# A conformer block on one core: the first feed-forward's up projection by seven block products, and its modulation vectors loaded later

## Chip, cores and metric

One core of a Trainium2 chip runs the kernel in one launch. The metric is device microseconds; the time of a kernel is the median over its runs. Rows of the profile come from one further execution, whose own time is given beside its span.

## What is computed

One layer on x of 512 tokens by 1024 features, all in float32 accuracy:

```python
ada = silu(c) @ w_ada + b_ada                # 9 modulation vectors of 1024
(sh1, sc1, g1, sh2, sc2, g2, sh3, sc3, g3) = split(ada, 9)
h = rmsnorm(x, ffn1_norm) * (1 + sc1) + sh1
x = x + 0.5 * g1 * swiglu(h, ffn1_w_in, ffn1_w_out)      # swiglu: (silu(h @ wg) * (h @ wu)) @ w_out
h = rmsnorm(x, mix_norm) * (1 + sc2) + sh2
z = h @ w_in      # latents of an MLA attention | q, k, v of a chunked attention | two gates
x = x + g2 * ((sigmoid(gA) * (mla @ w_branch_a) + sigmoid(gB) * (chunk @ w_branch_b)) @ w_out)
h = rmsnorm(x, ffn2_norm) * (1 + sc3) + sh3
x = x + 0.5 * g3 * swiglu(h, ffn2_w_in, ffn2_w_out)
return rmsnorm(x, final_norm)
```

The feed-forward is 2816 wide, so each up projection has 22 blocks f of 128 gate and 128 up columns. Vectors are counted 0 to 8 in the order above: 0 and 1 serve the first feed-forward, 2 is its gate; 4 and 3 are the mixer's scale and shift, 5 its gate; 7, 6 and 8 belong to the second feed-forward.

## The kernel before

**Products.** Every operand of a matmul is split into a high part (a cast on ACT, `split`, L196) and a low part (a subtraction on DVE, L197; in the mixer often on POOL), and every product is three matmuls, hi·hi, lo·hi, hi·lo (`mm3`, L212 to L214). Weights come as loads of 128x1024 (512 KB) into `raw`, a ring of five buffers, issued on SP's queue in the program's order (L191); their parts stand in a ring `wh`, `wl`.

**Stages.** The program goes through: the start, where vectors 0 and 1, the norm and F0 = 3 up blocks are made (`first_units`, order of all engines written by hand); the other 19 up blocks of the first feed-forward; its down projection; the mixer's norm; the mixer (latents, two attentions of 8 heads each, gates, output); the norm; two plain and 20 fast up blocks of the second feed-forward; its down projection and the last norm. Behind the start TensorE's order is the order of the code; the order of the other engines comes from a scheduler that goes by priorities, and each engine takes its instructions strictly in that order.

**Up blocks.** In the first feed-forward (`ffn_up`) a block is two units of 8 steps x 3 matmuls of 512 columns, 48 matmuls; behind each block `swiglu` (L502, L503) makes the activation and splits it at once. In the second one 20 blocks go through `up_fast`: the block matrix product of 2x2 in seven products instead of eight, 7 x 4 x 3 = 84 matmuls of 256 columns. Later products are added to PSUM sums that an ACT copy has seeded. Its price per block stands on DVE and ACT: three sums of weights (L612, L613, L616), splits of the sums, four copies and two silu (L624 to L638), three combinations (L632, L634, L641). It needs sums of the tokens too (`mix_tokens`). A third of its loads uses two free buffers of the gate rows and one of `ada`. Its activations stay unsplit and are split by `act_parts` in the down stage.

**Modulation vectors.** A vector is eight loads of 512 KB from `w_ada`, each followed by one DVE instruction: `ada_dot` (L287, with a short read) for shift and scale, `ada_step` (L283, adds to `ada_acc`) for a gate; a gate ends with `ada_rows` (a split, four matmuls with `ones`, L310 and L311, two ACT copies, L312). Vectors 2, 4, 3, 7, 6, 5 are streamed through the first up stage, one or two steps for each of 38 units; vector 8 through the second down stage.

**The mixer.** `Fill` hands out pieces of projection matmuls between the steps of the attention heads (`Head`, L74 to L107: a score bank, DVE L81, ACT exponential L83, DVE L84 and L85, transposes, a split by ACT L96 and DVE L97, values).

Of the kernel before, what the change touches and what calls it, by code (L numbers as in the profile page):

```python
# [18 lines left out]
P = 128  # L19
# [22 lines left out]
EARLY_UP, FLUSH_UP = 3, (0, 2)  # L42
F2 = 2
FLUSH_LAT = {0: 2, 1: 1}
# [75 lines left out]
class Fill:  # L120
    def __init__(self, ahead):
        self.jobs, self.ready, self.run, self.ahead = [], [], None, ahead

# [8 lines left out]
    def __call__(self, n):  # L132
        while n > 0:
            if self.run is None:
                self.look(1)
                if not self.ready:
                    return
                run, units = self.ready.pop(0)
                self.run = run(units)
                self.look(self.ahead)  # L140
            try:
                next(self.run)
                n -= 1
            except StopIteration:
                self.run = None
# [5 lines left out]
class Block:  # L151
# [115 lines left out]
    def mix_tokens(self, j):  # L267
        nc = self.nc
        ha, hb = self.mixed[2 * j:2 * j + 2]
        if not j:  # L270
            self.sums = [[self.slot([P, KT // 2, S // 2], F32R, "sum_" + p) for p in "hl"] for _ in range(4)]
        a11, a12, a21, a22 = (h[:, ks] for h in (ha, hb) for ks in (slice(0, 4), slice(4, 8)))
        tt = nc.vector.tensor_tensor
# [4 lines left out]
        cs = slice(j * P, (j + 1) * P)  # L278
        for (h, l), part in zip(self.sums, (a22, a11, a21, a12)):
            self.split(part, h[:, :, cs], l[:, :, cs])  # L280

# [32 lines left out]
    def ada_gate(self, vec):
        io, nc = self.io, self.nc
        layer = vec // 3
        acc = self.main.tile([P, D], F32, tag="ada", name="ada_acc", bufs=1)
        nc.gpsimd.memset(acc, 0.0)
        nc.scalar.dma_start(acc[0:1], io["b_ada"][:, vec * D:(vec + 1) * D])
        for j in range(KT):  # L320
            self.ada_step(acc, j, self.raw(D, io["w_ada"][vec, j]))
            yield j == KT - 1
        self.gate[layer] = self.fix.tile([P, D], F32, tag="gate", name="gate_bc", bufs=2)
        self.ada_rows(acc, self.gate[layer])
        yield True
# [50 lines left out]
    def first_units(self):  # L376
# [121 lines left out]

    def swiglu(self, psg, psu):
        nc = self.nc  # L500
        sc = self.sc4((P, 2, S))
        nc.scalar.activation(sc[:, 0], psg, AF.Silu)  # L502
        nc.vector.tensor_tensor(sc[:, 1], sc[:, 0], psu, op=ALU.mult)  # L503
        act = self.slot([P, 2, S], F32R, "act")
        self.split(sc[:, 1], act[:, 0], act[:, 1])
        return act

    def ffn_up(self, w1, fs, side):
        jobs = [(f, gu) for f in fs for gu in range(2)]
        ps, units, acts = {}, {}, []  # L510

        def mms(job, ns):
            hi, lo = units[job]
            for k in range(KT):
                cs = slice(k * P, (k + 1) * P)
                self.mm3(ps[job][:, ns], (hi[:, cs], lo[:, cs]), (self.hH[:, k, ns], self.hL[:, k, ns]),
                         k == 0, k == KT - 1)

        for i, job in enumerate(jobs):
            f, gu = job  # L520
            units[job] = self.unit(D, w1[f, gu])
            ps[job] = self.bank("o" if f % 2 and gu else "mm")
            mms(job, slice(0, S))
            while len(acts) < len(fs) and (fs[len(acts)], 1) in ps:
                n = fs[len(acts)]
                acts.append(self.swiglu(ps[n, 0], ps[n, 1]))
            side(i)
        return acts

    def act_tile(self, f):  # L530
# [3 lines left out]

    def up_plain(self, w1, fs, early, flush):
        nc = self.nc
        jobs = [(f, gu) for f in fs for gu in range(2)]
# [10 lines left out]
        for i, job in enumerate(jobs):  # L548
# [3 lines left out]
            if i < early:  # L552
# [5 lines left out]
                for late in jobs[:early]:  # L558
                    mms(late, S // 2, S)
                self.mix_tokens(0)  # L560
            else:
                mms(job, 0, S)
                if i == early:
                    self.mix_tokens(1)
            while done < len(fs) and (fs[done], 1) in ps:
                n = fs[done]
                sc = self.sc4((P, S))
                nc.scalar.activation(sc, ps[n, 0], AF.Silu)
                nc.vector.tensor_tensor(self.act_tile(n), sc, ps[n, 1], op=ALU.mult)
                done += 1  # L570

    def up_fast(self, w1, fs):
        nc = self.nc
# [22 lines left out]
        def load(n, i, src):  # L596
            m = (2 * n + i) % 7
# [310 lines left out]
    def mix(self, after):  # L908
        nc = self.nc
        self.fill = Fill(2)  # L910
# [139 lines left out]
    def layer(self, banks):  # L1050
        nc, io = self.nc, self.io
        acts = [self.swiglu(banks[2 * i], banks[2 * i + 1]) for i in range(F0)]
        self.rope_angles()
        gen = self.vectors((2, 4, 3, 7, 6, 5))
        acts += self.ffn_up(io["w1a"], range(F0, NF), lambda i: self.advance(gen, 1 + i % 2))
        for _ in range(3):
            self.advance(gen, 99)

        parts = lambda u: [[acts[2 * u + j][:, i] for i in range(2)] for j in range(2)]
        self.down(parts, NF, io["w2a"], 0, 3, lambda t, xn: self.norm_token(t, 1, xn), LAG_DOWN)  # L1060
        self.mix(lambda t, xn: self.norm_token(t, 2, xn))
# [33 lines left out]
def pack(inputs):  # L1095
# [17 lines left out]
    for tag, n in (("a", "ffn1"), ("b", "ffn2")):  # L1113
        w1 = a[n + "_w_in"][0].reshape(KT, P, 2, NF, P)
        both = w1.transpose(3, 2, 1, 0, 4).reshape(NF, 2, P, D)
        if tag == "b":
            q = w1.reshape(2, 4, P, 2, NF, P).transpose(4, 0, 3, 2, 1, 5)
            fast = np.stack([np.stack([q[:, 0, 0], q[:, 1, 1]], 2), np.stack([q[:, 1, 0], q[:, 0, 1]], 2)], 1)
            both = np.concatenate([both[:F2], fast.reshape(NF, 2, P, D)[F2:]])
        out["w1" + tag] = c(both)  # L1120
# [46 lines left out]
```

## Time and profile before

| | us |
|---|---|
| median of 3 runs (1115.17 to 1118.07) | 1115.86 |
| the profiled execution | 1115.35 |
| its span | 1113.6 |
| TensorE busy | 1084.4 |
| DVE busy | 700.7 |
| ACT busy | 525.1 |
| POOL busy | 134.7 |

Times inside the span are us from its start. TensorE's granted clock is full in all 40 slices of the span. "Busy" of an engine is time with an instruction in work; a matmul of 512 columns starts every 0.233 us, though its row shows 0.39, since matmuls overlap.

### The profile page before, as it was taken

Reading aid. Unit: us, or ns where it says so; the run is one execution under the profiler, and the core shown is the slowest. Engines: PE = TensorE matmul, PEld = TensorE weight load, DVE = VectorE, ACT = ScalarE, POOL = GpSimd, SP = SyncE. Lnnn points to the kernel's source line nnn. Section 1 sums busy time; section 2 is a strip of 40 time slices with the busy share of each in tenths; the row PEclk is TensorE's granted clock in tenths of the full one; section 3 lists DMA queues with packets and bytes.
Section 4 is the critical chain, followed back from the end, with each engine's and each line's share of the span. In section 5 each row is a group of like instructions: output and inputs, shape, how many; then the busy total and the mean of one; then the engine's idle time right before and its main releaser. Section 6 shows DMA issues by size and latency. Waiting matters only on the chain.

```text
span 1113.6 us, 15325 instructions
## 1 busy us (share of the span) xinstructions
PE 1084.4 (97%) x5884; PEld 925.4 (83%) x5884; DVE 700.7 (63%) x1170; ACT 525.1 (47%) x963; POOL 134.7 (12%) x126
## 2 busy tenths in 40 slices
PE   4999999999999999999999999999999999999997
PEld 3788888888888898988888788888999999988885
DVE  5887565663232575766677832459888787785724
ACT  5533232223122486766656633337555555654512
POOL 1000000000000011333343445100000000000100
PEclk9999999999999999999999999999999999999999
DMA  9677666663333630112222233623333333374312
GB/s 361 230 256 248 212 219 214 199 214 117 95 95 94 204 113 21 57 58 67 76 92 80 67 114 94 207 97 116 113 114 97 100 108 114 115 248 131 95 57 76
DMA packets 42993, 149.85 MB, mean 135 GB/s; under 512 B 5156, under 2 KB 5156, under 8 KB 42919
## 3 DMA queue, kind: packets, MB, share of 16 engines
q1 hardware_dynamic: 38160, 136.20, 37.3%
q10 hardware_dynamic: 4758, 12.66, 3.2%
q8 instruction: 46, 0.75, 0.3%
q14 instruction: 29, 0.23, 0.1%
HBM read 142.55 MB, written 6.29 MB: 134 GB/s over the span
## 4 chain that ended last, share of the span: by engine, by line
PE 90%; DVE 4%; ACT 3%; DMA 1%; issue 1%; ACTq 0%; POOLq 0%
PE ps_mm L212 14%; PE ps_mm L213 14%; PE ps_mm L214 14%; PE ps_s L213 3%; PE ps_s L214 3%; PE ps_s L212 3%; PE ps_o L214 3%; PE ps_o L212 3%; PE ps_o L213 3%; PE ps_s L586 3%; PE ps_s L587 3%; PE ps_s L588 3%; PE ps_t L212 2%; PE ps_t L214 2%; PE ps_t L213 2%; PE ps_t L586 2%
## 5 line engine op out<-in xcount | busy, mean ns | idle before, releaser
L196 ACT CAST wh<-raw 128x1024 fp32r<-128x1024 f32 x154 | 161.7, 1051 | 255.7 <-PE ps_t L214 73.5
L197 DVE TENSOR_TENSOR wl<-raw,wh 128x1024 fp32r<-128x1024 f32 x122 | 149.3, 1225 | 125.4 <-ACT wh L196 124.9
L212 PE MATMUL ps_mm<-h_hi,wh 128*128 128x512 f32 (+1 forms) x464 | 180.5, 389 | 0.0
L214 PE MATMUL ps_mm<-h_hi,wl 128*128 128x512 f32 (+1 forms) x464 | 177.9, 384 | 2.0 <-DVE wl L197 2.0
L213 PE MATMUL ps_mm<-h_lo,wh 128*128 128x512 f32 (+1 forms) x464 | 177.8, 383 | 0.2 <-DVE h_lo L197 0.2
L214 PEld LDWEIGHTS ps_mm<-h_hi,wl 128*128 128x128 f32 x464 | 87.2, 188 | 21.1 <-DVE wl L197 2.2
L213 PEld LDWEIGHTS ps_mm<-h_lo,wh 128*128 128x128 f32 x464 | 87.4, 188 | 16.3 <-DVE h_lo L197 0.4
L212 PEld LDWEIGHTS ps_mm<-h_hi,wh 128*128 128x128 f32 x464 | 87.4, 188 | 16.0
L197 POOL TENSOR_TENSOR wl<-raw,wh 128x1024 fp32r<-128x1024 f32 x32 | 77.1, 2413 | 81.2 <-ACT wh L196 81.2
L287 DVE CUSTOM_DVE_ANT_0 raw<-raw,c_row,cols_sb 128x1024 f32<-128x1024 f32 x32 | 41.0, 1284 | 46.5 <-DMA raw<-w_ada 46.4
L219 POOL TENSOR_TENSOR rstd<-ss,neghalf 128x1 f32<-128x1 f32 x16 | 10.4, 648 | 408.1 <-DVE ss L229 398.4
L83 ACT ACTIVATE sc<-sc,stat 128x128 f32<-128x128 f32 (+1 forms) x64 | 35.9, 562 | 29.2 <-DVE stat L81 29.0
L586 PE MATMUL ps_t<-sum_h,wh 128*128 128x256 f32 x160 | 44.8, 280 | 0.0
L588 PE MATMUL ps_t<-sum_h,wl 128*128 128x256 f32 x160 | 44.7, 279 | 0.0
L587 PE MATMUL ps_t<-sum_l,wh 128*128 128x256 f32 x160 | 44.7, 279 | 0.0
L587 PE MATMUL ps_s<-sum_l,wh 128*128 128x256 f32 x160 | 44.7, 279 | 0.0
L588 PE MATMUL ps_s<-sum_h,wl 128*128 128x256 f32 x160 | 44.7, 279 | 0.0
L586 PE MATMUL ps_s<-sum_h,wh 128*128 128x256 f32 x160 | 44.7, 279 | 0.0
L97 DVE TENSOR_TENSOR pt<-ps_t,pt 128x512 fp32r<-128x512 f32 (+1 forms) x64 | 30.9, 488 | 16.5 <-ACT pt L96 15.6
L283 DVE SCALAR_TENSOR_TENSOR ada_acc<-raw,cact,ada_acc 128x1024 f32<-128x1024 f32 x24 | 30.8, 1283 | 16.6 <-DMA raw<-w_ada 16.6
L196 ACT CAST act<-sc 128x512 fp32r<-128x512 f32 x22 | 13.6, 622 | 57.3 <-DVE sc L503 57.3
L197 DVE TENSOR_TENSOR act_l<-act,act_h 128x1024 fp32r<-128x1024 f32 x22 | 27.9, 1273 | 17.0 <-PE ps_t L213 15.9
(404 smaller groups left out, 2884.0 us busy)
## 6 DMA issues: line engine op xcount, KB each, us to landing
raw<-w_ada SPq DMA_DIRECT2D x56, 512.0 KB, 4.3
raw<-w1a SPq DMA_DIRECT2D x38, 512.0 KB, 4.2
raw<-w1b SPq DMA_DIRECT2D x28, 512.0 KB, 3.5
raw<-w2a SPq DMA_DIRECT2D x22, 512.0 KB, 3.5
raw<-w2b SPq DMA_DIRECT2D x22, 512.0 KB, 3.5
w_first<-w_first SPq DMA_DIRECT2D x16, 512.0 KB, 9.3
raw<-w_gate SPq DMA_DIRECT2D x16, 512.0 KB, 3.6
raw_g<-w1b SPq DMA_DIRECT2D x11, 512.0 KB, 3.5
```

Source lines behind the costliest of these rows:

```text
L83: nc.scalar.activation(p, p, AF.Exp, scale=-1.0, bias=low, accum_out=tot)
L97: nc.vector.tensor_tensor(pl[:, :n], pt[:, :n], ph[:, :n].bitcast(F32), op=ALU.subtract)
L196: nc.scalar.copy(hi, src)
L197: (low_engine or nc.vector).tensor_tensor(lo, src, hi.bitcast(F32), op=ALU.subtract)
L212: mm(ps, lh, rh, start=start, stop=False)
L213: mm(ps, lh, rl, start=False, stop=False)
L214: mm(ps, ll, rh, start=False, stop=stop)
L283: self.nc.vector.scalar_tensor_tensor(acc, w, self.cact[:, j:j + 1], acc, op0=ALU.mult, op1=ALU.add)
L287: self.nc.vector.tensor_tensor_reduce(w, w, self.c_row, 1.0, self.cols[:, b:b + 1], ALU.mult, ALU.add, out)
L586: mm(ps, hi[:, cs], lh, start=start and k == 0, stop=False, skip_group_check=not start)
L587: mm(ps, hi[:, cs], ll, start=False, stop=False, skip_group_check=not start)
L588: mm(ps, lo[:, cs], lh, start=False, stop=k == 3, skip_group_check=not start)
```

## The change

Of the first feed-forward's 19 up blocks two stay plain and 17 go through `up_fast`; the plain ones now use `up_plain`, and `mix_all` makes the token sums from `h32`, the modulated tokens, which are kept in the buffer that held x. So x is loaded a second time (`x_again`, four loads on ACT's queue) before the down stage, and its activations are split in the down stage by `act_parts`. In this `up_fast` loads use the five `raw` buffers for four in five and `ada` for one in five. Vector 2 is accumulated in its gate row, with one step behind each fast block from the sixth on; vectors 4 and 3 move to the down stage, one step for each of its units; vectors 7, 6 and 5 move to the mixer, one step at the start of each of Fill's jobs. `ada_rows` takes its split buffers from `wh` and `wl`. For vector 2 the DMA of its bias (L338 of the changed kernel) is issued in the start.

```diff
-F2 = 2
+F1, F2 = 2, 2
+WEIGHTS_A = ("raw",) * 4 + ("ada",)
+WEIGHTS_B = ("raw",) * 4 + ("gate",) * 2 + ("ada",)
...
-    def __init__(self, ahead):
-        self.jobs, self.ready, self.run, self.ahead = [], [], None, ahead
+    def __init__(self, ahead, side):
+        self.jobs, self.ready, self.run, self.ahead, self.side = [], [], None, ahead, side
...
+                self.side()
...
+    def sum_tiles(self):
+        self.sums = [[self.slot([P, KT // 2, S // 2], F32R, "sum_" + p) for p in "hl"] for _ in range(4)]
+
+    def mix_all(self):
+        self.sum_tiles()
+        h = self.halves(self.h32)
+        parts = [h[:, ks, :, b] for b in range(2) for ks in (slice(0, 4), slice(4, 8))]
+        self.token_sums(*parts, [[z.rearrange("p k (a c) -> p k a c", a=2) for z in pair] for pair in self.sums])
...
+    def gate_row(self, name="gate_bc"):
+        return self.fix.tile([P, D], F32, tag="gate", name=name, bufs=2)
+
+    def ada_rows(self, acc):
+        nc = self.nc
+        hi, lo = (self.ring.tile([P, D], F32R, tag="w" + p, name="gate_" + p) for p in "hl")
...
-            nc.scalar.mul(out[:, cs], ps, 0.5)
+            nc.scalar.mul(acc[:, cs], ps, 0.5)
...
-        acc = self.main.tile([P, D], F32, tag="ada", name="ada_acc", bufs=1)
+        if layer not in self.gate:
+            self.gate[layer] = self.gate_row()
+        acc = self.gate[layer]
...
-        self.gate[layer] = self.fix.tile([P, D], F32, tag="gate", name="gate_bc", bufs=2)
-        self.ada_rows(acc, self.gate[layer])
+        self.ada_rows(acc)
...
-        self.c_row = self.fix.tile([P, D], F32, tag="gate", name="c_row", bufs=2)
+        self.gate[0] = self.gate_row()
+        self.c_row = self.gate_row("c_row")
...
-            h32 = self.sc4((P, S)) if k < KT - 1 else self.main.tile([P, S], F32, tag="ada", name="h32", bufs=1)
+            h32 = self.h32[:, k]
...
+        self.h32 = self.fix.tile([P, KT, S], F32, tag="x16", name="h32")
...
-    def up_fast(self, w1, fs):
+    def up_fast(self, w1, fs, homes, side=None):
...
-            if m < 4:
+            home = homes[(2 * n + i) % len(homes)]
+            if home == "raw":
                 return self.raw(D, src)
-            if m < 6:
-                tile_ = self.fix.tile([P, D], F32, tag="gate", name="raw_g", bufs=2)
-            else:
-                tile_ = self.main.tile([P, D], F32, tag="ada", name="raw_a", bufs=1)
+            tile_ = self.gate_row("raw_g") if home == "gate" else self.main.tile([P, D], F32, tag="ada", name="raw_a", bufs=1)
...
+            if side:
+                side(n)
...
+        gen = self.vectors((7, 6, 5))
+        self.fill = Fill(2, lambda: self.advance(gen, 1))
         merged = self.attention()
+        for _ in range(3):
+            self.advance(gen, 99)
         self.low_engine = nc.vector
         self.x = self.fix.tile([P, NT, D], F32, tag="x16", name="x_back")
...
-        acts = [self.swiglu(banks[2 * i], banks[2 * i + 1]) for i in range(F0)]
+        self.acts = []
+        for f in range(F0):
+            self.swiglu(f, banks[2 * f], banks[2 * f + 1])
         self.rope_angles()
-        gen = self.vectors((2, 4, 3, 7, 6, 5))
-        acts += self.ffn_up(io["w1a"], range(F0, NF), lambda i: self.advance(gen, 1 + i % 2))
-        for _ in range(3):
-            self.advance(gen, 99)
-
-        parts = lambda u: [[acts[2 * u + j][:, i] for i in range(2)] for j in range(2)]
-        self.down(parts, NF, io["w2a"], 0, 3, lambda t, xn: self.norm_token(t, 1, xn), LAG_DOWN)
+        self.up_plain(io["w1a"], range(F0, F0 + F1), {0: self.mix_all})
+        gen = self.vectors((2,))
+        self.up_fast(io["w1a"], range(F0 + F1, NF), WEIGHTS_A, lambda n: self.advance(gen, n > 4))
+        self.x = self.fix.tile([P, NT, D], F32, tag="x16", name="x_again")
+        for t in range(NT):
+            nc.scalar.dma_start(self.x[:, t], io["x"][t * P:(t + 1) * P])
+        late = self.vectors((4, 3))
+        self.down(self.act_parts, NF, io["w2a"], 0, 3, lambda t, xn: self.norm_token(t, 1, xn), LAG_DOWN,
+                  side=lambda hf, u: self.advance(late, 1))
...
-        self.up_fast(io["w1b"], range(F2, NF))
-        fin = self.fix.tile([P, D], F32, tag="gate", name="final_gain", bufs=2)
+        mixes = {EARLY_UP + j - 1: lambda j=j: self.mix_tokens(j) for j in range(2)}
+        self.up_plain(io["w1b"], range(F2), mixes, EARLY_UP, FLUSH_UP)
+        self.up_fast(io["w1b"], range(F2, NF), WEIGHTS_B)
+        fin = self.gate_row("final_gain")
         nc.scalar.dma_start(fin, io["final"].to_broadcast([P, D]))
```

The host packs w1a accordingly (blocks from the sixth on in the order that `up_fast` reads).

Three places show the order of engines. The first is VectorE in the first up stage. Before (one plain block, with steps of vector 7, `adac`):

```order
165 L503 TENSOR_TENSOR sc_1122<-sc_1122,ps_mm 128x512
166 L197 TENSOR_TENSOR wl<-raw,wh 128x1024
167 L197 TENSOR_TENSOR act<-sc_1122,act 128x512
168 L287 ISA raw,adac<-raw,c_row,cols_sb 128x1024
169 L287 ISA adac 128x1
170 L197 TENSOR_TENSOR wl<-raw,wh 128x1024
171 L287 ISA raw,adac<-raw,c_row,cols_sb 128x1024
172 L287 ISA adac 128x1
```

The changed kernel, one fast block with a step of vector 2 (L297, the former L283); L599, L600 and L603 are the sums of weights, L619, L621 and L628 the combinations:

```order
203 L619 TENSOR_TENSOR sc_1781<-ps_t,sc_1781 128x256
204 L200 TENSOR_TENSOR wl<-raw,wh 128x1024
205 L200 TENSOR_TENSOR wl<-w_sums,wh 128x1024
206 L621 TENSOR_TENSOR sc_1781<-ps_s,sc_1781 128x256
207 L200 TENSOR_TENSOR wl<-raw,wh 128x1024
208 L628 TENSOR_TENSOR act<-sc_1781,sc_1872 128x2x2x128
209 L297 SCALAR_TENSOR_TENSOR gate_bc<-raw,cact,gate_bc 128x1024
210 L200 TENSOR_TENSOR w_last<-w_sums,w_last 128x512 x2
211 L599 TENSOR_TENSOR w_sums<-raw,raw_a 128x1024
```

The step stands ahead of the low part `w_last` of the next block and of the sums of the block behind it.

The second place is ScalarE where the up stage ends. Before, behind the last silu of the up stage (L502) come the casts for the down stage, whose activation halves are split already:

```order
129 L196 CAST wh<-raw 128x1024
130 L312 ACTIVATE gate_bc<-ps_t 128x512 x2
131 L502 ACTIVATE sc_1975<-ps_mm 128x512
132 L196 CAST wh<-raw 128x1024
133 L196 CAST act<-sc_1975 128x512
134 L196 CAST wh<-raw 128x1024 x10
```

The changed kernel (`sc_2747` belongs to the last block; L624 and L625 are its two silu):

```order
222 L1053 DMA x_again<-x 128x1024 x2
223 L618 COPY ps_o<-ps_s 128x256
224 L624 ACTIVATE sc_2747<-ps_mm 128x256
225 L1053 DMA x_again<-x 128x1024
226 L625 ACTIVATE sc_2747<-ps_o 128x256
227 L199 CAST wh<-raw 128x1024 x3
228 L199 CAST act_h<-act 128x1024 x3
```

The first weight of the down stage is now cast behind the second silu, which reads the last product's PSUM.

The third place is VectorE in the mixer, at the end of a head of the first attention. Before:

```order
468 L81 ISA sc_3683,stat<-ps_s,masks 128x512
469 L81 ISA stat 128x1
470 L84 RECIPROCAL stat<-stat 128x1
471 L85 TENSOR_SCALAR sc_3683<-sc_3683,stat 128x512
472 L114 TENSOR_TENSOR o_3213<-ps_o,o_3213 64x512
473 L968 TENSOR_TENSOR kT<-ps_t,kT 64x512
474 L978 TENSOR_TENSOR qT<-ps_t,qT 96x512
```

The changed kernel at the end of such a head, where vector 7 is finished (its last step is L301, the former L287):

```order
561 L83 ISA sc_4609,stat<-ps_s,masks 128x512
562 L83 ISA stat 128x1
563 L301 ISA raw,adac<-raw,c_row,cols_sb 128x1024
564 L301 ISA adac 128x1
565 L86 RECIPROCAL stat<-stat 128x1
566 L313 SCALAR_TENSOR_TENSOR scale_83<-adac,cols_sb 128x8
567 L87 TENSOR_SCALAR sc_4609<-sc_4609,stat 128x512
568 L116 TENSOR_TENSOR o_4130<-ps_o,o_4130 64x512
569 L960 TENSOR_TENSOR kT<-ps_t,kT 64x512
570 L970 TENSOR_TENSOR qT<-ps_t,qT 96x512
```

The step moved into the place where VectorE waits for the exponential, ahead of the reciprocal.

## Rows read from the trace of the kernel before

**Rows 1.** The page's first part: busy us, share of the span, instructions.

```profile
PE 1084.4 (97%) x5884; PEld 925.4 (83%) x5884; DVE 700.7 (63%) x1170; ACT 525.1 (47%) x963; POOL 134.7 (12%) x126
```

**Rows 2.** Windows: stretch, length, busy us by engine, clock, DMA share, GB/s.

```profile
57.20:271.80 214.60, 214.60 (x921) 172.94 (x920) 135.35 (x184) 66.35 (x89) 0.95 (x1) 1.00 0.65 213
271.80:388.00 116.20, 116.20 (x499) 93.51 (x498) 40.71 (x50) 31.31 (x41) 0.55 (x1) 1.00 0.37 116
437.00:650.00 213.00, 209.52 (x1179) 178.57 (x1178) 150.26 (x391) 140.41 (x329) 78.08 (x69) 1.00 0.22 70
861.00:881.00 20.00, 20.00 (x171) 19.77 (x170) 16.11 (x21) 11.36 (x20) 0.00 (x0) 1.00 0.36 104
```

**Rows 3.** Timeline of PE in the first up stage: start, us, instruction.

```profile
57.18 0.39 PE L212 MATMUL ps_mm<-h_hi,wh 128*128 128x512 f32 x1
...
96.38 0.39 PE L310 MATMUL ps_t<-sc,ones 128*128 128x512 f32 x1
...
271.83 0.40 PE L212 MATMUL ps_s<-wh,act 128*128 128x512 f32 x1
```

**Rows 4.** Timeline of PE: first and last fast matmul, start of the second down stage.

```profile
781.23 0.28 PE L586 MATMUL ps_s<-h_hi,wh 128*128 128x256 f32 x1
...
980.44 0.28 PE L588 MATMUL ps_o<-h_hi,w_last 128*128 128x256 f32 x1
...
981.95 0.50 PE L213 MATMUL ps_s<-wl,act_h 128*128 128x512 f32 x1 [0.76 <-DVE wl L197]
```

**Rows 5.** Groups by form, whole span: busy us, mean ns | idle before.

```profile
L197 DVE TENSOR_TENSOR wl<-raw,wh 128x1024 fp32r<-128x1024 f32 x122 | 149.3, 1225 | 125.4 <-ACT wh L196 124.9
L287 DVE CUSTOM_DVE_ANT_0 raw<-raw,c_row,cols_sb 128x1024 f32<-128x1024 f32 x32 | 41.0, 1284 | 46.5 <-DMA raw<-w_ada 46.4
L283 DVE SCALAR_TENSOR_TENSOR ada_acc<-raw,cact,ada_acc 128x1024 f32<-128x1024 f32 x24 | 30.8, 1283 | 16.6 <-DMA raw<-w_ada 16.6
...
L196 ACT CAST wh<-raw 128x1024 fp32r<-128x1024 f32 x154 | 161.7, 1051 | 255.7 <-PE ps_t L214 73.5 <-issue 62.5 <-PE ps_o L214 53.6
L638 ACT ACTIVATE sc<-ps_o 128x256 f32<-128x256 f32 x20 | 7.7, 384 | 7.4 <-PE ps_o L588 7.3
```

**Rows 6.** Timeline of DVE in a fast block, with PE's at 872.

```profile
869.16 1.23 DVE L197 TENSOR_TENSOR wl<-w_sums,wh 128x1024 fp32r<-128x1024 f32 x1 [0.17 <-ACT wh L196]
...
872.34 0.28 PE L586 MATMUL ps_t<-sum_h,wh 128*128 128x256 f32 x1
```

**Rows 7.** Start: piece of the chain that ended last; ACT's queue at 55.

```profile
8.03 1.06 ACT c_row L450
...
54.97 0.49 ACTq L319 DMA_DIRECT2D ada_acc<-b_ada  x1
```

**Rows 8.** DMA issues: KB each, median us to landing.

```profile
raw<-w_ada SPq DMA_DIRECT2D x56, 512.0 KB, 4.3
```

**Rows 9.** Timelines of POOL, DVE and PE in the mixer, from 447 to 639.

```profile
447.45 1.87 DVE L85 TENSOR_SCALAR sc<-sc,stat 128x512 f32<-128x512 f32 x1
...
480.42 4.74 POOL L197 TENSOR_TENSOR wl<-raw,wh 128x1024 fp32r<-128x1024 f32 x2 [5.37 <-ACT wh L196]
...
483.06 2.31 DVE L85 TENSOR_SCALAR sc<-sc,stat 128x384 f32<-128x384 f32 x1
...
485.76 0.39 PE L107 MATMUL ps_o<-pt,vs 128*128 128x256 f32 x1 [1.48 <-DVE pt L97]
...
579.38 2.39 POOL L197 TENSOR_TENSOR wl<-raw,wh 128x1024 fp32r<-128x1024 f32 x1
...
579.65 2.67 DVE L197 TENSOR_TENSOR o_hl<-o,o_hl 128x512 fp32r<-128x512 f32 x1 [0.18 <-ACT o_hl L196]
...
608.45 0.69 DVE L197 TENSOR_TENSOR o_hl<-o,o_hl 128x512 fp32r<-128x512 f32 x1 [0.69 <-ACT o_hl L196]
...
638.19 1.33 DVE L85 TENSOR_SCALAR sc<-sc,stat 128x256 f32<-128x256 f32 x1
```

**Rows 10.** Waits, 437 to 650: total us, times, longest.

```profile
DVE stat L84 <- ACT sc L83: 17.5, 27, 1.4
```

More of the change, by code (lines that the diff above doesn't have):

```diff
@@ L267, in mix_tokens, with token_sums @@
     def mix_tokens(self, j):
-        nc = self.nc
         ha, hb = self.mixed[2 * j:2 * j + 2]
         if not j:
-            self.sums = [[self.slot([P, KT // 2, S // 2], F32R, "sum_" + p) for p in "hl"] for _ in range(4)]
+            self.sum_tiles()
         a11, a12, a21, a22 = (h[:, ks] for h in (ha, hb) for ks in (slice(0, 4), slice(4, 8)))
-        tt = nc.vector.tensor_tensor
+        cs = slice(j * P, (j + 1) * P)
+        self.token_sums(a11, a12, a21, a22, [[z[:, :, cs] for z in pair] for pair in self.sums])
+    def token_sums(self, a11, a12, a21, a22, out):
+        tt = self.nc.vector.tensor_tensor
         tt(a22, a21, a22, op=ALU.add)
@@ L277, in mix_tokens @@
         tt(a12, a12, a11, op=ALU.subtract)
-        cs = slice(j * P, (j + 1) * P)
-        for (h, l), part in zip(self.sums, (a22, a11, a21, a12)):
-            self.split(part, h[:, :, cs], l[:, :, cs])
+        for (hi, lo), part in zip(out, (a22, a11, a21, a12)):
+            self.split(part, hi, lo)
+    def sum_tiles(self):
+        self.sums = [[self.slot([P, KT // 2, S // 2], F32R, "sum_" + p) for p in "hl"] for _ in range(4)]
+    def mix_all(self):
+        self.sum_tiles()
+        h = self.halves(self.h32)
+        parts = [h[:, ks, :, b] for b in range(2) for ks in (slice(0, 4), slice(4, 8))]
+        self.token_sums(*parts, [[z.rearrange("p k (a c) -> p k a c", a=2) for z in pair] for pair in self.sums])
     def ada_step(self, acc, j, w):
@@ L301, in ada_columns @@
         yield True
-    def ada_rows(self, acc, out):
+    def gate_row(self, name="gate_bc"):
+        return self.fix.tile([P, D], F32, tag="gate", name=name, bufs=2)
+    def ada_rows(self, acc):
         nc = self.nc
-        hi, lo = self.sc4(dtype=F32R), self.sc4(dtype=F32R)
+        hi, lo = (self.ring.tile([P, D], F32R, tag="w" + p, name="gate_" + p) for p in "hl")
         self.split(acc, hi, lo)
@@ L497, in first_units @@
         return banks
[L499 to L528, printed above, removed]
     def act_tile(self, f):
@@ L533, in act_tile, with swiglu, up_plain @@
         return self.acts[f // 2][:, f % 2]
-    def up_plain(self, w1, fs, early, flush):
-        nc = self.nc
+    def swiglu(self, f, psg, psu):
+        sc = self.sc4((P, S))
+        self.nc.scalar.activation(sc, psg, AF.Silu)
+        self.nc.vector.tensor_tensor(self.act_tile(f), sc, psu, op=ALU.mult)
+    def up_plain(self, w1, fs, mixes, early=0, flush=()):
         jobs = [(f, gu) for f in fs for gu in range(2)]
@@ L559, in up_plain @@
                     mms(late, S // 2, S)
-                self.mix_tokens(0)
             else:
                 mms(job, 0, S)
-                if i == early:
-                    self.mix_tokens(1)
+            if i in mixes:
+                mixes[i]()
             while done < len(fs) and (fs[done], 1) in ps:
                 n = fs[done]
-                sc = self.sc4((P, S))
-                nc.scalar.activation(sc, ps[n, 0], AF.Silu)
-                nc.vector.tensor_tensor(self.act_tile(n), sc, ps[n, 1], op=ALU.mult)
+                self.swiglu(n, ps[n, 0], ps[n, 1])
                 done += 1
-    def up_fast(self, w1, fs):
+    def up_fast(self, w1, fs, homes, side=None):
         nc = self.nc
@@ L596, in load @@
         def load(n, i, src):
-            m = (2 * n + i) % 7
-            if m < 4:
+            home = homes[(2 * n + i) % len(homes)]
+            if home == "raw":
                 return self.raw(D, src)
-            if m < 6:
-                tile_ = self.fix.tile([P, D], F32, tag="gate", name="raw_g", bufs=2)
-            else:
-                tile_ = self.main.tile([P, D], F32, tag="ada", name="raw_a", bufs=1)
+            tile_ = self.gate_row("raw_g") if home == "gate" else self.main.tile([P, D], F32, tag="ada", name="raw_a", bufs=1)
             nc.sync.dma_start(tile_, src)
@@ L909, in mix @@
         nc = self.nc
-        self.fill = Fill(2)
+        gen = self.vectors((7, 6, 5))
+        self.fill = Fill(2, lambda: self.advance(gen, 1))
         merged = self.attention()
+        for _ in range(3):
+            self.advance(gen, 99)
         self.low_engine = nc.vector
@@ L1074, in layer @@
             nc.scalar.dma_start(self.x_home[t], self.x[:, t])
-        self.up_plain(io["w1b"], range(F2), EARLY_UP, FLUSH_UP)
-        self.up_fast(io["w1b"], range(F2, NF))
-        fin = self.fix.tile([P, D], F32, tag="gate", name="final_gain", bufs=2)
+        mixes = {EARLY_UP + j - 1: lambda j=j: self.mix_tokens(j) for j in range(2)}
+        self.up_plain(io["w1b"], range(F2), mixes, EARLY_UP, FLUSH_UP)
+        self.up_fast(io["w1b"], range(F2, NF), WEIGHTS_B)
+        fin = self.gate_row("final_gain")
         nc.scalar.dma_start(fin, io["final"].to_broadcast([P, D]))
@@ L1115, in pack @@
         both = w1.transpose(3, 2, 1, 0, 4).reshape(NF, 2, P, D)
[L1116 to L1119, printed above, removed]
+        plain = F0 + F1 if tag == "a" else F2
+        q = w1.reshape(2, 4, P, 2, NF, P).transpose(4, 0, 3, 2, 1, 5)
+        fast = np.stack([np.stack([q[:, 0, 0], q[:, 1, 1]], 2), np.stack([q[:, 1, 0], q[:, 0, 1]], 2)], 1)
+        both = np.concatenate([both[:plain], fast.reshape(NF, 2, P, D)[plain:]])
         out["w1" + tag] = c(both)
```

## The prediction

> **What bounds the kernel now.** I read the page's first part, then windows by stage, then TensorE's timeline at the edges of the stages that the change touches, and last VectorE and ScalarE in those stages. TensorE is busy 1084.4 of 1113.6 us [rows 1], so the time can fall only by fewer TensorE cycles, and it rises by every wait that reaches TensorE. The reader should see in the windows that the two stages that change most differ in their reserve [rows 2]. In the first up stage TensorE never stops, VectorE works 135 of 215 us, and the granted clock is 1.00. In the mixer, 437 to 650, VectorE works 150.26 of 213 us beside POOL's 78.08 us, and TensorE already loses 213 − 209.52 = 3.5 us. All sums are made against the profiled execution's 1115.35 us, 0.5 below the median of 1115.86, so a forecast may be read on either scale with that half microsecond to spare.
>
> **The gain.** The first up stage runs from 57.18 to 271.83 [rows 3]. In it stand two groups of four matmuls with `ones` (one at 96.38), at the 0.233 us step of 512 columns 1.86 us in all. The rest, 212.79 us, is 19 plain blocks: 11.20 us each. The 20 fast blocks of the second feed-forward run from 781.23 to the last matmul at 980.44 and its own 0.12 us step [rows 4]: 199.33 us, 9.97 us each. The same 84 matmuls of the same shapes replace 48 here, so a block saves 1.23 us, and 17 save **21.0 us**. The `ones` matmuls are moved, not removed: nothing.
>
> **What takes time back.**
>
> *The start.* The bias DMA of vector 2 is now issued by ScalarE between c_row and the four squares, which the chain that ended last runs through; such an issue took 0.49 us, c_row 1.06 us [rows 7]. If the issue stands beside compute it is 0; I take **+0.4**. The POOL memset ahead of it has nothing to wait for.
>
> *The entry into the fast blocks.* `mix_all` (four sums, four splits on VectorE) lies beside the two plain blocks, 22 us of TensorE, with no vector steps there any more; the first fast weights need sums as well. Bounds 0 and one split with its cast, 2.3 us; I take **+0.3**, near the lower end, since VectorE keeps over a third of this stage free.
>
> *Vector 2 in the fast blocks.* In the steady state of the second feed-forward VectorE works 16.11 of 20 us [rows 2], 8.0 us per block of 9.97. A gate step of 1.283 us [rows 5] makes it 9.3: it fits, with 0.7 us left. Low parts there are done at 869.16 + 1.23 = 870.39 for a product that begins at 872.34 [rows 6], 1.95 us ahead, which also covers one step. But the step waits for its own load, which lands 4.3 us after issue [rows 8], and with five `raw` buffers 2.6 of every 3 loads now come through them instead of 1.1 of 2. The step stands ahead of `w_last` and of the next sums in VectorE's queue (first place of the order above), so a late load delays the weights that TensorE needs soonest. Eight steps cost between nothing and 8 x 1.283 = 10.3 us; I take a quarter, **+2.5**. The split for `ada_rows` takes a buffer pair from the weights' ring once: 0 to 2.3 us, I take **+0.5**.
>
> *From the up stage to the down stage.* In the second feed-forward the first weight of the down stage is cast before the last silu, and still its low part comes late: 980.44 to 981.95 [rows 4], 1.26 us above the step. Here ScalarE casts that weight behind the last silu (second place of the order). From the last matmul's end that is 0.38 us of silu, 1.05 of cast and 1.23 of low part [rows 5], with 0.3 for the hand-over and one matmul of 0.23 between: **+2.7**; bounds 1.26 and 3.5.
>
> *The down stage.* A unit is 24 matmuls, 5.6 us. VectorE gets a low part of the activations and a step of vectors 4 or 3: 1.23 + 1.23 + 1.28 = 3.7 us [rows 5]. Loads go from one to two in 5.6 us, where the DMA engines were busy 37% [rows 2]. Hidden: 0, as long as VectorE is not late by more than 1.9 us in a unit. x_again's four loads have all of this stage.
>
> *Vectors 7, 6 and 5 in the mixer.* 24 steps add 24 x 1.284 = 30.8 us to VectorE [rows 5], which must work in order. There is cover: before L84 VectorE waits for the exponential, 17.5 us over 27 times, 0.65 us each [rows 10], and the third place of the order shows a step put just there. 24 x 0.65 = 15.6 us may vanish so. There is also a further cost. At 579.65 VectorE's L197 took 2.67 us instead of the 0.69 at 608.45, and ended just behind POOL's L197, begun at 579.38; at 483.06 L85 took 2.31 us inside POOL's two operations from 480.42, and TensorE then waited 1.48 us for `pt` [rows 9]. So VectorE instructions stand still behind POOL's. From 447.45 to 638.19 twelve of 72 such rows (64 L85, 8 L197 `o_hl`) run at least 0.3 us over the shortest of their form, 13.7 us in all, 0.19 us for each of the 72: 24 steps would add 4.6 us. What reaches TensorE? At most its 3.5 us of lost time came of those 13.7 us of unplanned VectorE time: a quarter. A quarter of 30.8 + 4.6 − 15.6 = 19.8 us is **+5.0**. Bounds: 0, if priorities put all steps into waits, and all 35.4 us.
> The Trainium skill, page "SBUF — State Buffer", section "Who interferes with whom", says that a VectorE instruction with two SBUF inputs and a GpSimd instruction that reads SBUF exclude each other on a shared port, whichever comes first holding it to its end. The row at 579.65 agrees. A step has two SBUF inputs (weights, and c_row or the gate row); by that rule it would meet POOL 37% of the time for 1.2 us on average, 10.6 us in place of 4.6, and the sum would end 1.5 us higher.
>
> *Vector 5's row.* `ada_rows` now stands where the output projection runs: cast 1.05 us and low part 1.23 us [rows 5] in the weights' ring just ahead of their matmuls. I take **+2.0** of 2.3; 0 if TensorE has other work queued ahead.
>
> Sum: −21.0 + 0.4 + 0.3 + 2.5 + 0.5 + 2.7 + 2.0 + 5.0 = −7.6; 1115.35 − 7.6 = 1107.8, forecast **1108**.
>
> **Rivals.**
> A, slower: VectorE becomes the mixer's bound. 150.26 + 30.8 + 4.6 = 186 of 213 us leaves 13% of slack in an engine with many short handshakes; if all 35.4 us reach TensorE, the time is 1107.8 + 30.4 = 1138, if half, 1120. It decides from a mixer cost of 5.0 + 7.6 + 3.3 = 16 us on, 45% of the added work. For it: VectorE there already stands on TensorE's path [rows 9]. Against: the waits of [rows 10], and steps come only about every 9 us (24 in 213). Chance 0.11.
> B, the vectors are hidden everywhere: only the hand-over to the down stage and the start remain, 1115.35 − 21.0 + 2.7 + 0.4 = 1097.5 (1095 to 1102). For it: steps are late work with eight loads' time to spare; their idle cover exists in each stage. Against: 2.5 us per step is not free at every place in a strict order. Chance 0.20.
> C, the forecast: part of the mixer's work shows, 1102 to 1112.5. Chance 0.49.
> D, no measurable change: the mixer costs 10 to 16 us, or the gate steps cost their whole 10.3 us beside a mixer at 8: 1112.5 to 1119. Chance 0.20.
>
> **How the numbers follow.** A measurement of this kernel can tell about 0.3%, 3.3 us. Faster than 1112.5: B and C, 0.69. Within 1112.5 to 1119.2: D, 0.20. Slower: A, 0.11. The range of 8 in 10 leaves out A, the upper end of D and the lower half of B: 1098 to 1117. The likeliest case alone is 1102 to 1112.5.
>
> **What would show it.** Seventeen fast blocks at 9.97 us between 80 and 250: right; blocks six to thirteen above 10.2 with VectorE waiting for `w_ada` ahead of L297: the gate steps' term. A gap of about 2.7 us at the first matmuls of the down stage, with ScalarE's cast and VectorE's low part as releasers. No gaps in the down stage. In the mixer TensorE's lost time should rise from 3.5 to 8 or 9 us, with VectorE's instructions as releasers behind L301 and L297, and more VectorE instructions stretched beside POOL's L200. Wrong would make it above all that VectorE's order in the mixer is not what I price by a quarter: then rival A or B; or a start that ends more than 1 us later.

## The result and the profile after

The changed kernel takes 1131.08 us (median of 4 runs, 1129.48 to 1138.82), the kernel before 1116.94 beside it: ratio 1.0142, interval 1.0092 to 1.0191. It is slower; forecast was 1108, range 1098 to 1117. The profiled execution took 1129.48 us, 14.1 above that of before.

The page's first part and its chain of waits, for the changed kernel:

```profile
PE 1074.9 (95%) x6496; PEld 944.1 (84%) x6496; DVE 806.4 (72%) x1297; ACT 589.4 (52%) x1086; POOL 140.1 (12%) x126
...
PE 76%; DVE 9%; DMA 5%; ACT 5%; issue 2%; POOL 2%; ACTq 0%; POOLq 0%; DVEq 0%
```

TensorE is busy 9.5 us less than in [rows 1], and yet the span is longer: it waits more. In the chain that ended last, DMA has 5% of the span (the page names `raw<-w_ada` with 3%, some 34 us), VectorE 9%.

Windows of the changed kernel, columns as in [rows 2]: the up stage, the down stage, the mixer, and a stretch inside it:

```profile
57.20:251.80 194.60, 193.26 (x1529) 186.34 (x1527) 167.53 (x221) 109.42 (x189) 0.00 (x0) 1.00 0.41 134
251.80:369.40 117.60, 116.78 (x498) 93.39 (x498) 79.84 (x96) 50.47 (x62) 0.55 (x1) 1.00 0.58 184
420.50:650.00 229.50, 207.52 (x1127) 174.35 (x1128) 176.27 (x422) 137.01 (x322) 81.13 (x69) 0.97 0.35 113
...
520.00:527.00 7.00, 6.46 (x27) 5.56 (x28) 4.35 (x13) 4.06 (x9) 2.39 (x1) 0.76 0.47 147
```

The loss has one place. In the mixer TensorE now stands still for 229.50 − 207.52 = 22 us, against 3.5 in [rows 2], and at its lower clock for part of the rest. Three marks cut each kernel's profiled execution in the same way: the first matmul of the down stage, the first transposition of `q_tok` (mixer begins to attend) and the first matmul on `merged` (output projection).

| | time, us | first down matmul at | to `q_tok` | `q_tok` to `merged` |
|---|---|---|---|---|
| before | 1115.35 | 271.83 | 165.0 | 271.4 |
| changed | 1129.48 | 251.87 | 168.6 | 301.9 |

So 20.0 us were won by the down stage's first matmul, 3.6 given back up to the mixer, and 30.5 lost in it. Behind `merged` both run alike. (The first mark moves by itself: in e1 to e8, e12 and e13, whose code up to it is the changed kernel's, it lies between 252.3 and 254.3, so the 20.0 are the upper end of 17.5 to 20.)

One such loss, step by step, in the changed kernel: pieces of the chain that ended last, then what VectorE and TensorE did (timelines):

```profile
511.46 2.41 POOL wl L200
513.88 3.85 DMA raw<-w_ada
```

```profile
517.87 1.28 DVE L301 CUSTOM_DVE_ANT_0 raw<-raw,c_row,cols_sb 128x1024 f32<-128x1024 f32 x1 [3.19 <-DMA raw<-w_ada]
...
520.00 0.49 DVE L87 TENSOR_SCALAR sc<-sc,stat 128x512 f32<-128x512 f32 x1
...
520.54 0.33 PE L95 MATMUL ps_t<-ident,sc 128*128 128x128 f32 x1 [2.08 <-DVE sc L87]
...
522.83 0.63 PE L215 MATMUL ps_mm<-h_hi,wh 128*128 128x512 f32 x1
523.26 0.63 PE L216 MATMUL ps_mm<-h_lo,wh 128*128 128x512 f32 x1
```

POOL's low part of a weight ends at 513.87; only then a `raw` buffer is free, and SP issues the vector's load at once. It lands 3.85 us later. VectorE has stood idle for 3.19 us in front of the step, works 1.28 us on it, and only then comes to L86 and L87, the softmax that the transpositions wait for: TensorE waits 2.08 us. Behind it matmuls of 512 columns start 0.43 us apart instead of 0.233, the 1.2 GHz level; the mean granted clock of 520 to 527 was 0.76. In 510 to 520 TensorE had been busy 8.46 of 10 us. Some 20 matmuls of this kernel's mixer ran so, which is 4 of the 30 us. (Ahead of the prediction, and in it, `raw` is said to have five buffers. It has four; the fifth home of the fast blocks is `ada`.)

Ten of the 21 steps that run in the mixer waited so for their load, 16.5 us in all (VectorE's waits, 415 to 660: us in total, times, longest us):

```profile
DVE raw L301 <- DMA raw<-w_ada: 10.3, 6, 3.2
...
DVE gate_bc L297 <- DMA raw<-w_ada: 6.2, 4, 2.4
```

### The profile page after: what moved, and what is told of

Its sections match the earlier page's. It is cut to its first block, busy times and chain, and to the rows that moved or that the text cites. A ratio compares the mean times of both kernels' runs of the same rounds, so it can differ in the third digit from the quotient of the medians.

```text
span 1127.7 us, 16891 instructions
## 1 busy us (share of the span) xinstructions
PE 1074.9 (95%) x6496; PEld 944.1 (84%) x6496; DVE 806.4 (72%) x1297; ACT 589.4 (52%) x1086; POOL 140.1 (12%) x126
## 4 chain that ended last, share of the span: by engine, by line
PE 76%; DVE 9%; DMA 5%; ACT 5%; issue 2%; POOL 2%; ACTq 0%; POOLq 0%; DVEq 0%
PE ps_mm L215 7%; PE ps_mm L216 7%; PE ps_mm L217 7%; PE ps_s L578 5%; PE ps_s L576 5%; PE ps_s L577 5%; DMA raw<-w_ada 3%; PE ps_t L578 3%; PE ps_t L577 3%; PE ps_t L576 3%; PE ps_s L216 2%; PE ps_s L217 2%; PE ps_s L215 2%; PE ps_t L215 2%; PE ps_t L216 2%
## 5 line engine op out<-in xcount | busy, mean ns | idle before, releaser
L200 DVE TENSOR_TENSOR wl<-raw,wh 128x1024 fp32r<-128x1024 f32 x116 | 142.4, 1230 | 67.6 <-ACT wh L199 67.4
L215 PE MATMUL ps_mm<-h_hi,wh 128*128 128x512 f32 (+1 forms) x264 | 103.3, 391 | 0.0
L217 PE MATMUL ps_mm<-h_hi,wl 128*128 128x512 f32 (+1 forms) x264 | 100.5, 381 | 1.9 <-DVE wl L200 1.9
L216 PE MATMUL ps_mm<-h_lo,wh 128*128 128x512 f32 (+1 forms) x264 | 100.5, 381 | 0.2 <-DVE h_lo L200 0.2
L200 POOL TENSOR_TENSOR wl<-raw,wh 128x1024 fp32r<-128x1024 f32 x32 | 77.6, 2428 | 84.9 <-ACT wh L199 84.8
L578 PE MATMUL ps_s<-sum_h,wl 128*128 128x256 f32 x296 | 82.8, 280 | 0.0
L578 PE MATMUL ps_t<-sum_h,wl 128*128 128x256 f32 x296 | 82.7, 279 | 0.0
L577 PE MATMUL ps_t<-sum_l,wh 128*128 128x256 f32 x296 | 82.7, 279 | 0.0
L577 PE MATMUL ps_s<-sum_l,wh 128*128 128x256 f32 x296 | 82.6, 279 | 0.0
L200 DVE TENSOR_TENSOR act_l<-act,act_h 128x1024 fp32r<-128x1024 f32 x44 | 53.2, 1221 | 23.8 <-PE ps_t L216 20.2
L578 PEld LDWEIGHTS ps_s<-sum_h,wl 128*128 128x128 f32 x296 | 55.6, 188 | 0.1
L301 DVE CUSTOM_DVE_ANT_0 raw<-raw,c_row,cols_sb 128x1024 f32<-128x1024 f32 x32 | 41.0, 1281 | 20.6 <-DMA raw<-w_ada 18.3
L576 PEld LDWEIGHTS ps_t<-sum_h,wh 128*128 128x128 f32 x296 | 55.7, 188 | 0.0
L577 PEld LDWEIGHTS ps_t<-sum_l,wh 128*128 128x128 f32 x296 | 55.6, 188 | 0.0
```

Source lines behind the costliest of these rows:

```text
L200: (low_engine or nc.vector).tensor_tensor(lo, src, hi.bitcast(F32), op=ALU.subtract)
L215: mm(ps, lh, rh, start=start, stop=False)
L216: mm(ps, lh, rl, start=False, stop=False)
L217: mm(ps, ll, rh, start=False, stop=stop)
L301: self.nc.vector.tensor_tensor_reduce(w, w, self.c_row, 1.0, self.cols[:, b:b + 1], ALU.mult, ALU.add, out)
L576: mm(ps, hi[:, cs], lh, start=start and k == 0, stop=False, skip_group_check=not start)
```

## Experiments

All are variants of the changed kernel; their edits are shortened to the lines that matter. "Mixer" is the stretch from `q_tok` to `merged`. e1, e2, e3, e7 and e12 were run once, and their times are that one profiled execution.

**e1, no vectors in the mixer.**

```diff
-        gen = self.vectors((7, 6, 5))
-        self.fill = Fill(2, lambda: self.advance(gen, 1))
+        self.fill = Fill(2, lambda: None)     # shift[2], scale[2], gate[1] by memset
```

> Leaves out vectors 7, 6 and 5 wholly (their results are constants): no loads, no steps, no gate row in the mixer. Late loads: the mixer falls back to what it was, 33 us off the changed kernel's 1129.5, so about 1097. VectorE's occupation: the same 1097, since the steps are gone too. If it stays above 1110, neither theory has the place right and the loss lies outside the mixer.

Measured 1099.59; mixer 272.4 us, near before's 271.4. The loss is that of the vectors in the mixer; all else of the change is worth 16 us against before's 1115.35.

**e2, steps without loads; e3, loads with short steps; e4, loads in other buffers.**

```diff
 e2: -  self.raw(D, io["w_ada"][vec, m])        + self.once      # vectors 5, 6, 7
 e3: +  w, c_row = w[:, :8], c_row[:, :8]       # in the mixer
 e4: -  self.raw(D, io["w_ada"][vec, m])        + w = self.slot([P, D], F32, "ada_w"), sync.dma_start
```

> All 24 steps stay in the mixer at full size, but all read one tile that is loaded once, so 23 of the 24 loads are left out (and the three vectors are not those of the reference). Late loads: 1100 to 1106, as only 31 us of VectorE work without a wait for a load remain. VectorE's occupation: still 1122 to 1130.

> All 24 loads stay, through the same ring of raw buffers, but each step works on 8 of its 1024 columns (so most of the three products is left out). Late loads: the waits stay, 1115 to 1127. VectorE's occupation: 1098 to 1102.

> All the work of the changed kernel; only the buffer of the mixer's 24 loads is another, from the ring of 22 slots instead of the four raw buffers that the weights share. Late loads: the issue no longer waits for POOL's low part of a weight, 1100 to 1108. VectorE's occupation: unchanged, 1125 to 1132.

e2 took 1103.63, which looked like a verdict for late loads alone. It isn't one. With nothing to wait for, the scheduler had moved the steps out of the heads:

```profile
L301 DVE CUSTOM_DVE_ANT_0 once<-once,c_row,cols_sb x16: 1276/1285/1286, 331.4 to 359.7; 128x1024 f32<-128x1024 f32 x16
...
L297 DVE SCALAR_TENSOR_TENSOR gate_bc<-once,cact,gate_bc x8: 1267/1278/1360, 409.8 to 428.4; 128x1024 f32<-128x1024 f32 x8
```

(source view of e2: ns min/median/max, first and last start). Sixteen steps ran in the down stage and eight ahead of most heads, so e2 shows only that steps in those places are nearly free. e3 took 1116.75, mixer 289.8: 17 us above e1's though the steps are short. e4 took 1124.50 (ratio to before 1.0076, 1.0047 to 1.0105), far above its expectation. Its timelines show one reason:

```profile
529.42 11.21 SPq L194 DMA_DIRECT2D raw<-w_ca  x2
540.72 0.38 SPq L308 DMA_DIRECT2D ada_w<-w_ada  x1
...
545.17 1.28 DVE L301 CUSTOM_DVE_ANT_0 ada_w<-ada_w,c_row,cols_sb 128x1024 f32<-128x1024 f32 x1 [0.81 <-DMA ada_w<-w_ada]
```

The vector's load needs no `raw` buffer any more, but it stands in SP's queue behind a weight's load that does, and is issued only after it (POOL's low part, 537.87 to 540.27, frees that buffer). But late loads are the smaller part of what e4 still loses: only 3 of its 23 steps in the mixer waited for a load, 6.8 us in all, against 16.5 us in the changed kernel. The rest is seen in e5.

**e5, slots and two jobs ahead; e6, slots and ScalarE's queue; e7, `raw` and one job ahead; e8, vectors 7 and 6 in the down stage.**

```diff
 e5: +  while self.todo and len(self.got) <= 2:
     +      self.got.append(self.slot([P, D], F32, "ada_w")); sync.dma_start(self.got[-1], next load)
     +  return self.got.pop(0)
 e6: the same with <= 0 and scalar.dma_start
 e7: the same with <= 1 and self.raw
 e8: late = self.vectors((4, 3, 7, 6)), advance(late, 2); vector 5 as in e5
```

> The kernel with the slot buffers, and each of the 24 loads issued two of Fill's jobs before its step, on the same queue of SP. Late by the queue's order (in e4 a load still stood behind a weight's load that waited for POOL): 1101 to 1107, 4 above the kernel without loads at most. Late by buffers (slots run short, as raw buffers did): no better than e4's 1124.5. VectorE's occupation: also 1124.

> The kernel with the slot buffers, its 24 loads issued by ScalarE's queue instead of SP's, not ahead. Late by the queue's order: the loads pass SP's weights, 1103 to 1112, with up to 24 issues of some 0.35 us on ScalarE, which works two thirds of the mixer. Late by buffers: about 1124.

> The 24 loads stay in the four raw buffers, but each is issued one job ahead of its step, so a raw buffer is held for a whole job. Late by the queue's order alone: 1103 to 1112. Late by buffers: the weights now wait for the buffer that the vector holds, 1120 to 1140.

> Vectors 4, 3, 7 and 6 in the first down stage, two steps per unit through the raw buffers; only vector 5's eight steps stay in the mixer, in slots and two jobs ahead. A down unit then has 1.23 + 1.23 + 2 x 1.28 = 5.0 us of VectorE in 5.6 us of TensorE and three loads. Late by the queue's order or VectorE's occupation alike: if the down stage hides this, 1100 to 1104; if three loads through four raw buffers are too many there, each of 20 units loses about 1 us: 1120.

e5: 1116.46, ratio 1.0004 (0.9993 to 1.0014), mixer 289.3; its steps waited for a load once, 1.3 us. e6: 1127.49 (ratio 1.0103, 1.0086 to 1.0120), and e7: 1131.17; neither another queue (e6 against e4) nor an issue one job earlier in the old buffers helps. Against the changed kernel's 1131.08 buffers of its own gave 6.6 us (e4), and with an earlier issue 14.6 (e5); two jobs ahead in the old buffers was not tried. But e5 is not at 1107 either. What is left is seen in its timelines of POOL, VectorE and TensorE:

```profile
614.50 2.36 POOL L200 TENSOR_TENSOR wl<-raw,wh 128x1024 fp32r<-128x1024 f32 x1 [2.98 <-ACT wh L199]
...
615.26 2.68 DVE L297 SCALAR_TENSOR_TENSOR gate_bc<-ada_w,cact,gate_bc 128x1024 f32<-128x1024 f32 x1
617.86 0.67 DVE L87 TENSOR_SCALAR sc<-sc,stat 128x512 f32<-128x512 f32 x1
...
618.59 0.33 PE L95 MATMUL ps_t<-ident,sc 128*128 128x128 f32 x1 [3.11 <-DVE sc L87]
```

No load is late here. The step itself stands between the reciprocal and L87, is stretched from 1.28 to 2.68 us beside POOL's L200, and TensorE waits 3.11 us. The row agrees with the rule of the shared port that the prediction took from the Trainium skill ("SBUF — State Buffer", "Who interferes with whom"): a step has two SBUF inputs, and POOL's subtraction, begun first, reads SBUF.

e8: 1117.57, ratio 1.0008. Its mixer is 275.5, but the way to it 180.2: with two steps per unit one step waited for its load in front of the down stage's first low part, and TensorE waited 6.7 us there and 2.2 and 0.6 us at the stage's end (374); behind both its clock was at the lower level for some us, which makes up most of the rest.

**e12, e5 with short steps; e13, e5 eight jobs ahead.**

```diff
 e12: e5 with the short steps of e3        e13: e5 with <= 8
```

> e5 (loads in slots, two jobs ahead) with each step cut to 8 of 1024 columns, so most of three products is left out. e5 still loses 17 us in the mixer although its steps hardly wait for loads. If that is the steps' own 1.28 us in places where VectorE's next instructions are urgent: 1101 to 1106. If it is the loads (traffic, slots, SP's queue): 1112 to 1117.

> e5 with loads issued eight jobs ahead instead of two, all work in place. If the place of a step is what costs (e2's 24 steps without loads ran at 409 to 430, ahead of the attention heads, and cost 4 us): more steps come early, 1106 to 1113. If slots or traffic: e5's 1116 or above.

e12: 1105.35, mixer 276.9. This makes a square, mixer in us:

| | load late (`raw`) | load ahead (slots) |
|---|---|---|
| full step | 301.9 (changed) | 289.3 (e5) |
| short step | 289.8 (e3) | 276.9 (e12) |

Late loads cost 12.6 and 12.9 us, the steps themselves 12.5 and 12.2, and the two add up. Each cell is one execution: by their whole times the late loads cost 11.0 and 11.4 us and the steps 12.7 and 13.1, and by the medians (1131.08 and 1116.46) late loads cost 14.6, so read late loads as 11 to 15 us and the steps as 12 to 13. A change of loads or steps also moved the steps to other places and changed what TensorE lost to its lower clock (some 4 us in the changed kernel, none in e3), which is not separated here. e12's 4.4 above e1 lie in vector 5's row (from the first value matmul of the last head to `merged` 68.6 us against 63.8): 24 loads and short steps alone cost nothing, so traffic is not what the mixer lost. e13: 1115.41 (ratio 0.9979, 0.9965 to 0.9994), above its expectation though the mixer took 281.4, down from 289.3, as nine steps now ran at 409 to 422; they stand among the rope instructions of `q_tok` and `kT`, for which TensorE then waited 5.3 us at 419: 3.2 us more than in e5 on the way to `q_tok`.

**e10, spread over the stages; e14 and e15, one edge of it mended; e16, both.** Vector 5 is treated as in e5, alone in the mixer. Vectors 2 and 7 go into the fast blocks, 4, 3 and 6 into the down stage.

```diff
 e10: gen = self.vectors((2, 7)), 1 step per fast block; late = self.vectors((4, 3, 6)), 1 per down unit, rest behind
 e14: e10, three steps in the plain blocks, fast blocks n < 15
 e15: one generator (2, 7, 4, 3, 6): fast blocks n < 15, each down unit, rest behind
 e16: e10 with lambda n: self.advance(gen, 2 if n in (4, 7, 10) else n < 15)
```

> All work in place: vectors 2 and 7 in the fast blocks, one step in each of the 17; vectors 4, 3 and 6 in the down stage, one step per unit, the rest of 6 behind its last unit; vector 5's eight steps alone in the mixer, in slots, two jobs ahead. If both a late load and the place of a step cost only in the mixer: 1101 to 1107, below both kernels. If steps in the first fast blocks or behind the down stage cost as in the mixer: 1112 or more.

> e10 with vectors 2 and 7 begun three units earlier, in the plain blocks, so that their last load and step are over two fast blocks before the down stage. e10 lost 8 us at the entry to the down stage, where the first weight's low part stood behind a step that waited for its load. If that is the raw buffers and VectorE's queue being full at this edge: 1106 to 1109, with a gap under 3 us there. If the edge is late for another reason: 1114 to 1117 again.

> All work in place, vector 5's steps alone in the mixer as in e10. One row of steps through the stages, 2, 7, 4, 3, 6: one in each of the first 15 fast blocks, none in the plain blocks (where e14 lost 6 us) and none in the last two fast blocks (where e10 lost 8 us), one in each of the 22 down units, seven behind them. If those two edges were all that e10 and e14 lost beside the mixer's part: 1106 to 1110. If steps behind the down stage cost 1.3 us each in front of the mixer's norm: 1112 or more.

> e14's down stage and mixer, with all 16 steps of vectors 2 and 7 in the first 15 fast blocks, two steps in some: all work in place. A block with two steps has 8.0 + 2.6 = 10.6 us of VectorE in 9.97 of TensorE, but its weights are 1.95 us ahead. If a step costs only where VectorE has no slack ahead of TensorE: the up stage ends near 254, as e10's did, without e10's 6 us gap, and the time is 1106 to 1110. If double steps are late: 1112 or more.

| | median, us | ratio to before, interval | first down matmul | to `q_tok` | to `merged` |
|---|---|---|---|---|---|
| e10 | 1115.63 | 0.9985, 0.9974 to 0.9997 | 253.4 | 177.0 | 277.0 |
| e14 | 1112.74 | 0.9961, 0.9949 to 0.9973 | 260.0 | 169.7 | 275.5 |
| e15 | 1114.32 | 0.9970, 0.9955 to 0.9984 | 253.8 | 175.8 | 276.9 |
| e16 | 1109.84 | 0.9943, 0.9923 to 0.9964 | 253.5 | 171.4 | 277.2 |

The mixer was mended in all four, to 3 to 5 us above e1's. The rest went mostly at edges. VectorE and TensorE of e10 at the entry to the down stage:

```profile
257.04 1.28 DVE L301 CUSTOM_DVE_ANT_0 raw<-raw,c_row,cols_sb 128x1024 f32<-128x1024 f32 x1 [5.77 <-DMA raw<-w_ada]
...
259.85 0.79 PE L216 MATMUL ps_s<-wl,act_h 128*128 128x512 f32 x1 [5.92 <-DVE wl L200]
```

Once more a step waits for its load, and a weight's low part stands behind it. The load is late for another reason than in the mixer, though: it was issued at 249.83, 7.2 us ahead, and until 257 the DMA engines were busy 89% (35% in the changed kernel's mixer), with `x_again`'s four loads issued at 246.8 to 250.7 among their work. A later `x_again` was not tried. e14 ended this, but VectorE then worked without a break from 62.5 on, in the plain blocks, on token sums and rope angles, a weight's low part came late, and TensorE lost 3.0 us at 72 and ran at the lower clock behind it (the plain blocks took 27.2 us against 22.4); which change of the order did it was not traced. e15 missed its expectation around the end of the down stage, where its seven last steps ran (357 to 371): TensorE waited 1.4 us at 367, and in the norm behind it 2.9 us at 393, released by ScalarE; what joins the two was not traced. e16 has neither edge and is the fastest: 0.6% below the kernel before, where the changed kernel is 1.4% above. Its way to `q_tok` is still 5 us longer than e1's 166.2, with waits of 1.4 and 1.3 us at 367 and 385.

## Why the prediction was wrong, step by step

- **The gain** was right: 79.59 to 250.30, without the four `ones` matmuls (0.93 us), is 169.8 us for 17 blocks, 9.99 each with the steps of vector 2 in them, forecast 9.97 without.
- **The start and the entry** cost nothing that shows (forecast 0.4 and 0.3): the up stage begins at 57.20 against 57.18 in [rows 3] (56.8 to 58.0 in the runs with the same start), and two plain blocks later, at 79.59, the first fast one. **Vector 2 in the fast blocks** cost 0.3 us in all here, forecast 3.0. That is the lowest of eleven executions of this code: e1 to e8, e12 and e13 took 170.4 to 171.7 us for the 17 blocks, 0.9 to 2.2 above 169.5, with one step waiting up to 2.0 us for its load around 183. So 3.0 was too high, and the term isn't nothing.
- **From up to down** was forecast at 2.7 us. TensorE's timeline of the changed kernel:

```profile
250.18 0.28 PE L578 MATMUL ps_o<-h_hi,w_last 128*128 128x256 f32 x1
251.87 0.50 PE L215 MATMUL ps_s<-wh,act_h 128*128 128x512 f32 x1 [1.41 <-ACT wh L199]
253.12 0.50 PE L216 MATMUL ps_s<-wl,act_h 128*128 128x512 f32 x1 [0.76 <-DVE wl L200]
```

That is 1.57 + 1.02 = 2.6 us, by the releasers that were named. (The lower bound, 1.26, was read a little high: 1.51 less the steps of 0.12 and 0.23 is 1.16.)
- **The down stage** was forecast at nothing. From the second down matmul to `q_tok` the changed kernel is 2.6 us longer; 1.7 of it lie in the latents at 379 to 420, where the first steps of vector 7 now run (e1, without them, is as quick there as before).
- **The mixer's vectors** are the step that failed. "24 steps add 24 x 1.284 = 30.8 us to VectorE", at a quarter of 19.8 us, +5.0: they cost 25, in two halves that the square shows.
  The first half was left out. I priced late loads in the fast blocks, where they cost 2 us at most, and not in the mixer, where they cost 12.6 to 12.9 us. The reason stood in a row that I had used for another point, POOL's L197 of 2.39 us [rows 9]: in the mixer a `raw` buffer is held until POOL's low part is done, and the vectors' loads, in the same ring and the same queue, are issued only then, 3.9 us ahead of the earliest moment at which VectorE can go on.
  The second half was mis-sized. The steps by themselves cost 12.2 to 12.5 us, 40% of their 30.8, not a quarter of what was left after a cover of 15.6. (Three of the 24 run ahead of `q_tok`, and a short step still takes 0.22 us: between e5 and e12 VectorE's steps in the mixer fell from 33.6 to 10.2 us, and half of that reached TensorE.) The cover was wrong: a step put "just there", where VectorE waits 0.65 us for the exponential, is twice as long as that wait, and L87 behind it is what TensorE needs next. The stretching beside POOL, forecast at 4.6 us, came out at 6.6 us on seven steps in e5 (2.2 on one in the changed kernel, where most steps start late), between the 4.6 and the 10.6 that the prediction gives; the size was fair, the share that reaches TensorE was not.
- **Vector 5's row** was forecast at 2.0. At the mark `merged` the changed kernel lost 3.2 us (67.0 against 63.8 from the first value matmul of the last head), of which 0.93 are the moved `ones` matmuls: 2.3.
- **The rivals.** A came true, from its point of decision (16 us) on, at 1129.5 between the 1120 and 1138 that were given for a half and all of the work; but its reason, VectorE as the bound of the mixer, is only half of it. VectorE was busy 176 of 229.5 us there. It was not short of time; it stood still for loads, and did the steps ahead of more urgent work.

## What to carry to other kernels

A load that is moved is not hidden because the DMA engines are idle: ask which buffer it takes, who frees that buffer and how late, what stands ahead of it in its queue, and what else loads at that moment; here it needed its own buffers and an issue two jobs ahead, 14.6 us together, of which the buffers alone gave 6.6. An instruction that is put into an engine's strict order is not covered by that engine's average idle time, but by the single wait in front of which it stands: 1.28 us in a wait of 0.65, ahead of what the busiest engine needs next, cost 40% of its length or more, and little (0.3 to 2.2 us for eight steps) in the fast blocks, where low parts are made two microseconds ahead. When an experiment takes a wait away, look where the scheduler has put the instruction before reading its time: e2 answered another question than the one it was made for.

## What was not expected of the hardware

Short waits can have a price beyond themselves. After stalls of the changed kernel's mixer TensorE's matmuls of 512 columns started 0.43 us apart for 3 to 7 us: the mean granted clock was 0.76 in 520 to 527, 0.72 in 590 to 596 and 0.67 in 645 to 655; over 420.5 to 650 it was 0.97, and 1.00 in [rows 2]. How long TensorE stands still in all doesn't decide it. In e3 it stood still for 18 us in the mixer and the clock stayed 1.00; in e12 it stood still for 5.6 us, and the clock of 650 to 655 was 0.66, behind two waits of 0.96 and 0.76 us. Nor does one short wait: at the entry to the down stage the same two waits (1.41 and 0.76 us) were followed by a clock of 0.66 over 254 to 259 in e5 and e12, and of 1.00 over 255 to 260 in e3. What sets it off stays open here.
